# A float32 decoder trunk on Trainium2: token factors in the turning matmuls, norm weights in the split

## The chip, the cores and the metric

The kernel runs on one core of a Trainium2 chip. The metric is the device time of one execution in microseconds; lower is better. The core has TensorE (PE; its weight loads are shown apart as PEld), VectorE (DVE), ScalarE (ACT), GpSimd (POOL) and SyncE (SP), which here issues the DMAs.

## What is computed

Four residual layers over 512 tokens of 1024 channels, all in float32. Each layer has a token mixer (retention in layers 0 and 3, a Conformer convolution in layer 1, a short convolution in layer 2) and a squared-ReLU MLP, and each of these eight sublayers has an RMSNorm before and one after it:

```python
def rms_norm(x, g):
    xf = x.astype(F32)
    y = xf * lax.rsqrt(jnp.mean(xf * xf, axis=-1, keepdims=True) + RMS_EPS)
    return (y * g.astype(F32)).astype(x.dtype)

def squared_relu_mlp(x, w1, w2):
    return jnp.square(jax.nn.relu(x @ w1)) @ w2

    for i in range(DEPTH):
        kind, j = i % N_MIXERS, i // N_MIXERS
        h = rms_norm(x, norm_g[i, 0])
        if kind == 0:
            h = retention_mixer(h, positions, ret_w_in[j], ret_gn_g[j], ret_w_out[j])
        ...
        x = x + rms_norm(h, norm_g[i, 1])
        h = squared_relu_mlp(rms_norm(x, norm_g[i, 2]), mlp_w1[i], mlp_w2[i])
        x = x + rms_norm(h, norm_g[i, 3])
```

The matrix products keep float32 accuracy by splitting: every operand is a high part, rounded to the matmul's reduced float32, and a low part, the rest. A product is three matmuls (high by high, high by low, low by high).

## The kernel before

Weights come from DRAM in pieces of 128 x 1024 (`load`, tile `raw`, two buffers). `fetch_hi` rounds a piece on ScalarE into `whi`, and `fetch_lo` takes the rest on VectorE into `wlo` and asks for the next piece; seven pieces fit. `settle` makes fetches that are owed, at most as many as it is told.

The activations `x` lie with 128 tokens on the partitions, in four token blocks. A mixer or MLP needs them with the channels on the partitions, in `xin`, as high and low parts. The way from one sublayer to the next, a boundary, is `out_final`. Its first half makes channels 0 to 511 of the sublayer's output for all four token blocks. The second half is `block(b)` for token block b: 24 matmuls of 128x512 over four weight pieces. Around these calls the code writes out by hand what follows for each token block b: the evacuation of the product into `f` (`evac`), its square sum on ScalarE (`square`), `post_norm` (the factor 1/rms through `rstd`, two small GpSimd steps, and `fold`, the product of `f` and the norm weights on VectorE), `add` (x gets f times the factor), `pre_sum` (square sum of x and its factor), `pre_norm` (L434: x times the factor, by token, times the norm weights, by channel, into `bnd`), `transposes` (L445: eight 128x128 transposes of `bnd` on TensorE, into two PSUM banks) and `place` (the split of these banks into `xin`: L376 on ScalarE, L377 on VectorE, each twice 128x512).

`first_four` begins the next sublayer. It takes its first four weight pieces and makes the products for tokens 0 to 255 in eight steps of twelve 128x256 matmuls (two steps a piece); before step T2_AT it turns token block 2, before step T3_AT block 3. Then follow tokens 256 to 511. The last boundary of the program has no next sublayer. The start of the program (`build`) does the same work on the input x: twenty warm-up matmuls (`warm`, L237), then the turning of blocks 0 and 1, and blocks 2 and 3 within `first_four`. The norm weights arrive as a row that a DMA broadcasts to all partitions (`begin_boundary`).

Each engine runs its instructions in the order in which the code issues them: nothing is reordered except inside the Conformer mixer, which has a planner of its own. PSUM has eight banks, taken in turn.

Of the kernel before, what the change touches and what calls it, by code (L numbers as in the profile page):

```python
# [16 lines left out]
P = 128  # L17
# [27 lines left out]
T2_AT, T3_AT, FETCH_AT = 3, 7, 3  # L45
# [17 lines left out]
O_PH = O_INV + 1  # L63
# [137 lines left out]
class Trunk:  # L201
# [200 lines left out]
    def begin_boundary(self, post, pre):  # L402

        nc = self.nc
        t = self.big.tile([P, 4, D], F32, tag="bnd", name=self.nm("bnd"))
        if post is not None:
            nc.sync.dma_start(t[:, 0, :], self.norm_g[post[0], post[1]:post[1] + 1, :].broadcast_to([P, D]))
        if pre is not None:
            nc.sync.dma_start(t[:, 1, :], self.norm_g[pre[0], pre[1]:pre[1] + 1, :].broadcast_to([P, D]))
            self.xin = self.big.tile([P, 2, 8, S], F32R, tag="xin", name=self.nm("xin"))  # L410
        self.bnd = t
# [10 lines left out]
    def post_norm(self, b):  # L422
        self.r1[b] = self.rstd(self.sums[b])
        self.fold(b)
# [5 lines left out]
    def pre_sum(self, b):  # L430
        self.r2[b] = self.rstd([self.sumsq(self.x[:, b, :], self.bnd[:, 2 + b % 2, :])])

    def pre_norm(self, b):
        self.nc.vector.scalar_tensor_tensor(self.bnd[:, 2 + b % 2, :], self.x[:, b, :], self.r2[b],  # L434
                                            self.bnd[:, 1, :], op0=ALU.mult, op1=ALU.mult)

    def transposes(self, b):
        nc = self.nc
        h = self.bnd[:, 2 + b % 2, :]
        self.turned[b] = []  # L440
        for m in range(2):
            bk = self.bank().rearrange("p (k t) -> p k t", k=4)
            for k in range(4):
                d0 = (4 * m + k) * P
                nc.tensor.transpose(out=bk[:, k, :], in_=h[:, d0:d0 + P], identity=self.ident)  # L445
            self.turned[b].append(bk)

    def place(self, b):
        c = slice(b * P, (b + 1) * P)
        for m, bk in enumerate(self.turned.pop(b)):  # L450
            self.split(self.xin[:, 0, 4 * m:4 * m + 4, c], self.xin[:, 1, 4 * m:4 * m + 4, c], bk)
# [51 lines left out]
    def out_final(self, slots, mode, layer_end):  # L503
# [86 lines left out]
        self.transposes(0)  # L590
        square(2, 1)
        self.pre_norm(1)
        self.place(0)
        self.post_norm(2)
        block(3, range(3))
        self.transposes(1)
        self.add(2)
        self.place(1)
        if layer_end:
            layer_end(2)  # L600
        self.pre_sum(2)
        block(3, range(3, 4))
# [4 lines left out]
        post(3)  # L607

        def start(i):
            if i == T2_AT:  # L610
                self.transposes(2)
                if FETCH_AT & 1:
                    self.settle(1)
                self.place(2)
                self.pre_sum(3)
                self.pre_norm(3)
                if FETCH_AT & 2:
                    self.settle(1)
            elif i == T3_AT:
                self.transposes(3)  # L620
                self.place(3)
# [745 lines left out]
    def build(self):  # L1367
        tc, nc = self.tc, self.nc
        SP = bass.MemorySpace.PSUM if hasattr(bass, "MemorySpace") else bass.MemoryType.PSUM
        with tc.tile_pool(name="const", bufs=1) as cp, tc.tile_pool(name="big", bufs=1) as big, \  # L1370
# [13 lines left out]
            self.r1, self.r2, self.turned = {}, {}, {}  # L1384
# [3 lines left out]
            self.begin_boundary(None, (LAYERS[0], 0))  # L1388
            self.load()
# [4 lines left out]
            self.small = cp.tile([P, O_PH], F32, name="small")  # L1394
            nc.sync.dma_start(self.small, self.small_in[:, :O_PH])
# [8 lines left out]
            def head(b):  # L1404
                self.r2[b] = self.rstd([self.sumsq(self.x[:, b, :], self.f[:, b, :])])

            def start(i):
                if i == S2_AT:
                    self.transposes(2)
                    self.place(2)  # L1410
                    self.pre_norm(3)
                elif i == S3_AT:
                    self.transposes(3)
                    self.place(3)
# [11 lines left out]
            self.place(1)  # L1426
# [49 lines left out]
def lay_out(inputs):  # L1476
# [41 lines left out]
    small[:, O_PH:] = phases.reshape(-1, P).T  # L1518
    small[:, O_INV] = (10000.0 ** e.astype(np.float64)).astype(np.float32)
# [25 lines left out]
```

## Time and profile before

| | us |
|---|---|
| median of 3 runs | 2544.07 (2544.06 to 2546.12) |
| the profiled execution | 2545.85 |
| its span | 2544.1 |
| TensorE busy | 2516.4 |
| VectorE busy | 1652.9 |
| ScalarE busy | 1210.3 |
| GpSimd busy | 218.4 |

The span runs from the first to the last instruction of the profiled execution. Busy time is the sum of the stretches in which an engine has an instruction running; matmuls overlap, and their ends are modelled, so the distance between two starts says what a matmul costs in a row. The granted TensorE clock is 0.998 of full speed over the span.

### The profile page before, as it was taken

What the parts mean: (1) busy time and instruction counts of PE and PEld (TensorE: products, weight loads), DVE (VectorE), ACT (ScalarE), POOL (GpSimd) and SP (SyncE); (2) the same over time, 40 slices, a digit from 0 to 9 for tenths busy, and PEclk for the clock granted to TensorE, in tenths of its full rate; (3) what the DMA queues carried; (4) which work ended last, traced back from release to release, by engine and by line L of the source; (5) the groups of instructions that cost most, each with busy time, mean ns of one, the idle gap of its engine ahead of it and who ended that gap; (6) DMA issues with size and microseconds to landing.
All of it is one profiled execution on the core that took longest, in us unless ns stands there. A gap on an engine that the chain in (4) does not pass through costs nothing. (4 is left out here: it accounts for less than half of the span.)

```text
span 2544.1 us, 30985 instructions
## 1 busy us (share of the span) xinstructions
PE 2516.4 (99%) x12173; PEld 2124.6 (84%) x12173; DVE 1652.9 (65%) x2151; ACT 1210.3 (48%) x1829; POOL 218.4 (9%) x248
## 2 busy tenths in 40 slices
PE   9999999999999999999999999999999999999998
PEld 8888888888888788888888888888888888888887
DVE  7665346897758977677464476784646534677773
ACT  3543444555436656544332365444344334455542
POOL 1000002000027820000010100000100000200000
PEclk9999999999999999999999999999999999999999
DMA  4323234224423532332332333314322223421331
GB/s 160 104 88 109 78 127 172 97 102 170 153 92 108 188 128 100 124 133 91 116 100 99 108 116 133 133 52 155 128 79 80 95 90 106 162 106 67 133 124 67
DMA packets 85026, 290.94 MB, mean 114 GB/s; under 512 B 9488, under 2 KB 11280, under 8 KB 84880
## 3 DMA queue, kind: packets, MB, share of 16 engines
q1 hardware_dynamic: 84880, 288.96, 32.7%
q8 instruction: 95, 1.56, 0.2%
q14 instruction: 51, 0.42, 0.0%
HBM read 265.79 MB, written 21.50 MB: 113 GB/s over the span
## 5 line engine op out<-in xcount | busy, mean ns | idle before, releaser
L337 PE MATMUL bank<-xin,whi 128*128 128x512 f32 (+1 forms) x2112 | 753.3, 365 | 2.3 <-ACT xin L376 2.3
L338 PE MATMUL bank<-xin,wlo 128*128 128x512 f32 (+1 forms) x2112 | 750.3, 364 | 0.0
L282 DVE TENSOR_TENSOR wlo<-raw,whi 128x1024 fp32r<-128x1024 f32 x340 | 416.8, 1234 | 426.5 <-ACT whi L271 425.2
L271 ACT ACTIVATE whi<-raw 128x1024 fp32r<-128x1024 f32 x340 | 354.8, 1053 | 428.9 <-DMA raw<-wall 214.7
L340 PE MATMUL bank<-xin,whi 128*128 128x512 f32 (+1 forms) x2112 | 473.8, 364 | 3.2 <-DVE xin L377 3.2
L337 PEld LDWEIGHTS bank<-xin,whi 128*128 128x128 f32 x2112 | 398.9, 189 | 65.0 <-ACT xin L376 2.9
L338 PEld LDWEIGHTS bank<-xin,wlo 128*128 128x128 f32 x2112 | 399.0, 189 | 62.2
L340 PEld LDWEIGHTS bank<-xin,whi 128*128 128x128 f32 x2112 | 369.3, 189 | 67.1 <-DVE xin L377 4.8
L266 ACT ACTIVATE whi<-blk 128x1024 fp32r<-128x1024 f32 x168 | 174.5, 1053 | 123.1 <-DVE blk L303 117.0
L280 DVE TENSOR_TENSOR wlo<-blk,whi 128x1024 fp32r<-128x1024 f32 x168 | 204.8, 1221 | 19.9 <-ACT whi L266 18.7
L396 POOL TENSOR_SCALAR tiny<-tiny,tiny 128x1 f32<-128x1 f32 x32 | 52.3, 1635 | 1484.7 <-ACT tmp L415 1483.5
L1200 ACT ACTIVATE tmp<-bank 128x512 f32<-128x512 f32 x128 | 75.2, 588 | 133.0 <-PE bank L340 133.0
L1287 DVE TENSOR_TENSOR f<-f,bank 128x512 f32<-128x512 f32 x168 | 108.4, 681 | 0.0
L1067 POOL TENSOR_TENSOR pbuf<-pbuf 128x512 f32<-128x512 f32 x69 | 100.5, 1473 | 16.0 <-ACT pbuf L1064 12.7
L327 PE MATMUL bank<-whi,hid 128*128 128x512 f32 (+1 forms) x264 | 101.5, 385 | 0.0
L329 PE MATMUL bank<-whi,hid 128*128 128x512 f32 (+1 forms) x264 | 101.0, 383 | 0.0
L328 PE MATMUL bank<-wlo,hid 128*128 128x512 f32 (+1 forms) x264 | 101.0, 383 | 0.0
L327 PE MATMUL bank<-whi,y 128*128 128x512 f32 x256 | 99.9, 390 | 0.0
L327 PE MATMUL bank<-whi,xin 128*128 128x512 f32 x256 | 99.6, 389 | 0.0
L329 PE MATMUL bank<-whi,y 128*128 128x512 f32 x256 | 99.6, 389 | 0.0
L328 PE MATMUL bank<-wlo,y 128*128 128x512 f32 x256 | 99.6, 389 | 0.0
L328 PE MATMUL bank<-wlo,xin 128*128 128x512 f32 x256 | 99.6, 389 | 0.0
(224 smaller groups left out, 4135.6 us busy)
## 6 DMA issues: line engine op xcount, KB each, us to landing
raw<-wall SPq DMA_DIRECT2D x340, 512.0 KB, 3.3
blk<-wall SPq DMA_DIRECT2D x96, 512.0 KB, 5.4
park<-x SPq DMA_DIRECT2D x20, 512.0 KB, 2.6
x<-park SPq DMA_DIRECT2D x20, 512.0 KB, 4.5
bnd<-norm_g SPq DMA_DIRECT2D x16, 512.0 KB, 6.8
phase<-tmp SPq DMA_DIRECT2D x32, 256.0 KB, 2.0
x<-x_in SPq DMA_DIRECT2D x8, 512.0 KB, 6.5
whi<-phase SPq DMA_DIRECT2D x8, 512.0 KB, 6.9
```

The source lines that it names most:

```text
L266: nc.scalar.activation(hi, self.form_of(c, n), AF.Copy)
L271: nc.scalar.activation(hi, self.raws[i], AF.Copy)
L280: nc.vector.tensor_sub(lo, self.form_of(c, n), hi.bitcast(F32))
L282: nc.vector.tensor_sub(lo, self.raws.pop(i), hi.bitcast(F32))
L327: nc.tensor.matmul(out, ah, bh, start=start, stop=False)
L328: nc.tensor.matmul(out, ah, bl, start=False, stop=False)
L329: nc.tensor.matmul(out, al, bh, start=False, stop=stop)
L337: self.nc.tensor.matmul(out, wh[:, c], x, start=kt == 0, stop=False)
L338: self.nc.tensor.matmul(out, wl[:, c], x, start=False, stop=False)
L340: self.nc.tensor.matmul(out, wh[:, kt * P:(kt + 1) * P], self.xin[:, 1, kt, t0:t1], start=False, stop=kt == 7)
L1067: nc.gpsimd.tensor_tensor(accs[c], accs[c], pbuf[:, slot, :], op=ALU.add)
L1287: nc.vector.tensor_add(f, f, bank)
```

## The change

`pre_norm` no longer scales x. It multiplies the 128x128 identity by the factors of the 128 tokens and leaves this diagonal matrix in `bnd`. `transposes` becomes eight float32 matmuls with x as the stationary and the diagonal matrix as the moving operand, which turns and scales x at once. The norm weights are now one column per 128 channels in the table `small`, and `place` multiplies by them while it splits, now for two token blocks together: eight ScalarE and eight VectorE passes of 128x256, from four banks. `begin_boundary` loads no norm row for this any more, and the start loads `small` earlier. The order in `out_final` is new, and so are the steps of `first_four` at which blocks 2 and 3 are turned. `post_norm` calls `fold` ahead of `rstd`, and the factor of `pre_sum` moves into `pre_norm`.

```diff
-T2_AT, T3_AT, FETCH_AT = 3, 7, 3
+T2_AT, T3_AT = 2, 5
...
-            nc.sync.dma_start(t[:, 1, :], self.norm_g[pre[0], pre[1]:pre[1] + 1, :].broadcast_to([P, D]))
+
+            self.gain = O_G + 16 * pre[0] + 4 * pre[1]
...
     def post_norm(self, b):
+        self.fold(b)
         self.r1[b] = self.rstd(self.sums[b])
-        self.fold(b)
...
     def pre_sum(self, b):
-        self.r2[b] = self.rstd([self.sumsq(self.x[:, b, :], self.bnd[:, 2 + b % 2, :])])
+        self.sums2[b] = self.sumsq(self.x[:, b, :], self.bnd[:, 2, :])
 
     def pre_norm(self, b):
-        self.nc.vector.scalar_tensor_tensor(self.bnd[:, 2 + b % 2, :], self.x[:, b, :], self.r2[b],
-                                            self.bnd[:, 1, :], op0=ALU.mult, op1=ALU.mult)
+
+        r = self.rstd([self.sums2.pop(b)])
+        self.diag[b] = self.bnd[:, 3, b * P:(b + 1) * P]
+        self.nc.vector.tensor_scalar(self.diag[b], self.ident, r, None, op0=ALU.mult)
 
     def transposes(self, b):
-        nc = self.nc
-        h = self.bnd[:, 2 + b % 2, :]
-        self.turned[b] = []
-        for m in range(2):
-            bk = self.bank().rearrange("p (k t) -> p k t", k=4)
-            for k in range(4):
-                d0 = (4 * m + k) * P
-                nc.tensor.transpose(out=bk[:, k, :], in_=h[:, d0:d0 + P], identity=self.ident)
-            self.turned[b].append(bk)
-
-    def place(self, b):
-        c = slice(b * P, (b + 1) * P)
-        for m, bk in enumerate(self.turned.pop(b)):
-            self.split(self.xin[:, 0, 4 * m:4 * m + 4, c], self.xin[:, 1, 4 * m:4 * m + 4, c], bk)
+
+        if b % 2 == 0:
+            self.turned[b // 2] = [self.bank().rearrange("p (k t) -> p k t", k=2) for _ in range(4)]
+        t = slice(b % 2 * P, b % 2 * P + P)
+        for k in range(8):
+            self.nc.tensor.matmul(self.turned[b // 2][k // 2][:, k % 2, t], self.x[:, b, k * P:(k + 1) * P], self.diag[b],
+                                  start=True, stop=True)
+
+    def place(self, n):
+
+        c = slice(256 * n, 256 * n + 256)
+        for k in range(8):
+            v, g = self.turned[n][k // 2][:, k % 2, :], self.small[:, self.gain + k:self.gain + k + 1]
+            hi = self.xin[:, 0, k, c]
+            self.nc.scalar.activation(hi, v, AF.Copy, scale=g)
+            self.nc.vector.scalar_tensor_tensor(self.xin[:, 1, k, c], v, g, hi.bitcast(F32), op0=ALU.mult, op1=ALU.subtract)
...
         evac(2, 1, ends[2])
-        self.transposes(0)
         square(2, 1)
         self.pre_norm(1)
+        post(2)
+        self.pre_sum(2)
+        block(3, range(1))
+        self.transposes(0)
+        self.transposes(1)
         self.place(0)
-        self.post_norm(2)
-        block(3, range(3))
-        self.transposes(1)
-        self.add(2)
-        self.place(1)
-        if layer_end:
-            layer_end(2)
-        self.pre_sum(2)
-        block(3, range(3, 4))
+        block(3, range(1, 4))
         self.owed += 4
         evac(3, 1, ends[3])
         square(3, 1)
         self.pre_norm(2)
         post(3)
+        self.pre_sum(3)
...
             if i == T2_AT:
                 self.transposes(2)
-                if FETCH_AT & 1:
-                    self.settle(1)
-                self.place(2)
-                self.pre_sum(3)
+                self.settle(1)
                 self.pre_norm(3)
-                if FETCH_AT & 2:
-                    self.settle(1)
+                self.settle(1)
             elif i == T3_AT:
                 self.transposes(3)
-                self.place(3)
+                self.place(1)
```

What this makes of the engines' order is shown at the first inner boundary (retention of layer 0 to its MLP). First TensorE, where the turning of block 0 stands; the 128x512 rows belong to `block(2)` and `block(3)`. Before:

```order
L328 MATMUL bank_3180<-wlo_2984,y_2716 128x512
L329 MATMUL bank_3180<-whi_2983,y_2716 128x512
L445 MATMUL bank_3206<-ident,bnd_2945 128x128 x4
L445 MATMUL bank_3211<-ident,bnd_2945 128x128 x4
L327 MATMUL bank_3229<-whi_2842,y_2302 128x512
```

After, `bnd` being the diagonal:

```order
L447 MATMUL bank_3240<-bnd_2960,x_2954 128x128 x2
L447 MATMUL bank_3241<-bnd_2960,x_2954 128x128 x2
L447 MATMUL bank_3242<-bnd_2960,x_2954 128x128 x2
L447 MATMUL bank_3243<-bnd_2960,x_2954 128x128 x2
L447 MATMUL bank_3240<-bnd_2960,x_2954 128x128 x2
L447 MATMUL bank_3241<-bnd_2960,x_2954 128x128 x2
L447 MATMUL bank_3242<-bnd_2960,x_2954 128x128 x2
L447 MATMUL bank_3243<-bnd_2960,x_2954 128x128 x2
L328 MATMUL bank_3233<-whi_2899,y_2317 128x512
```

The turnings of blocks 0 and 1 now stand together, after the first six matmuls of block 3.

VectorE at the same place: L515 and L521 are evacuations, L420 and L422 folds, L428 and L430 adds, L282 and L283 low parts of weights. Before, from the scaling of block 1 on:

```order
L434 SCALAR_TENSOR_TENSOR bnd_2945<-x_2939,tiny_3177,bnd_2945 128x1024
L377 TENSOR_TENSOR xin_2948<-bank_3206,xin_2948 128x4x128
L377 TENSOR_TENSOR xin_2948<-bank_3211,xin_2948 128x4x128
L420 TENSOR_TENSOR f_2045<-f_2045,bnd_2945 128x1024
L428 SCALAR_TENSOR_TENSOR x_2939<-f_2045,tiny_3225,x_2939 128x1024
L377 TENSOR_TENSOR xin_2948<-bank_3248,xin_2948 128x4x128
L377 TENSOR_TENSOR xin_2948<-bank_3253,xin_2948 128x4x128
L515 TENSOR_TENSOR f_2045<-f_2045,bank_3229 128x512
L434 SCALAR_TENSOR_TENSOR bnd_2945<-x_2939,tiny_3267,bnd_2945 128x1024
```

After, from the diagonal of block 1 on, with the last diagonal (block 3) at the end:

```order
L439 TENSOR_SCALAR bnd_2960<-ident,tiny_3220 128x128
L422 TENSOR_TENSOR f_2060<-f_2060,bnd_2960 128x1024
L430 SCALAR_TENSOR_TENSOR x_2954<-f_2060,tiny_3226,x_2954 128x1024
...
L457 SCALAR_TENSOR_TENSOR xin_2962<-bank_3243,small,xin_2962 128x256 x2
L521 TENSOR_TENSOR f_2060<-f_2060,bank_3233 128x512
L439 TENSOR_SCALAR bnd_2960<-ident,tiny_3299 128x128
L422 TENSOR_TENSOR f_2060<-f_2060,bnd_2960 128x1024
L430 SCALAR_TENSOR_TENSOR x_2954<-f_2060,tiny_3305,x_2954 128x1024
L283 TENSOR_TENSOR wlo_3318<-raw_3061,whi_3317 128x1024
L283 TENSOR_TENSOR wlo_3364<-raw_3091,whi_3363 128x1024
L439 TENSOR_SCALAR bnd_2960<-ident,tiny_3370 128x128
```

The fold and the add of block 2 have moved ahead of the split of blocks 0 and 1, and the evacuation of block 3 is behind all of that split.

ScalarE: L415 and L417 are square sums (of `f` with 512 columns, of `x` with 1024), L271 and L272 roundings of weights. Before, from the square sum of x of block 2 on:

```order
L415 ACTIVATE bnd_2945,tiny_3264<-x_2939 128x1024
L415 ACTIVATE tmp_3277,tiny_3278<-f_2045 128x512
L271 ACTIVATE whi_3293<-raw_3047 128x1024
L271 ACTIVATE whi_3349<-raw_3077 128x1024
L376 ACTIVATE xin_2948<-bank_3339 128x4x128
L376 ACTIVATE xin_2948<-bank_3344 128x4x128
L415 ACTIVATE bnd_2945,tiny_3359<-x_2939 128x1024
```

After, from the same square sum on:

```order
L417 ACTIVATE bnd_2960,tiny_3231<-x_2954 128x1024
L456 ACTIVATE xin_2962<-bank_3240,small 128x256 x2
L456 ACTIVATE xin_2962<-bank_3241,small 128x256 x2
L456 ACTIVATE xin_2962<-bank_3242,small 128x256 x2
L456 ACTIVATE xin_2962<-bank_3243,small 128x256 x2
L417 ACTIVATE tmp_3295,tiny_3296<-f_2060 128x512
L417 ACTIVATE bnd_2960,tiny_3310<-x_2954 128x1024
L272 ACTIVATE whi_3317<-raw_3061 128x1024
L272 ACTIVATE whi_3363<-raw_3091 128x1024
```

The split of blocks 0 and 1 stands behind the square sum of block 2, and the two roundings behind that of block 3.

## Rows read from the trace of the kernel before

**Rows 1.** The page's first block: busy us, share of span, instructions.

```profile
PE 2516.4 (99%) x12173; PEld 2124.6 (84%) x12173; DVE 1652.9 (65%) x2151; ACT 1210.3 (48%) x1829; POOL 218.4 (9%) x248
```

**Rows 2.** TensorE by shape: line, op, out<-in, shapes, count; busy us, mean ns; idle.

```profile
L445 PE MATMUL bank<-ident,bnd 128*128 128x128 f32 x256 | 33.5, 274 | 8.3 <-DVE bnd L434 8.2
...
L718 PE MATMUL bank<-ends 128*128 128x128 f32 x32 | 4.8, 274 | 0.0
```

**Rows 3.** TensorE's timeline: start us, us to the last end, line, shapes, count.

```profile
409.64 1.03 PE L445 MATMUL bank<-ident,bnd 128*128 128x128 f32 x8
...
410.98 0.39 PE L329 MATMUL bank<-whi,y 128*128 128x512 f32 x1
411.21 0.39 PE L327 MATMUL bank<-whi,y 128*128 128x512 f32 x1
...
887.95 5.07 PE L237 MATMUL bank<-ident 128*128 128x128 f32 x44
```

**Rows 4.** By stretch: length, busy us (instructions) by engine, clock, DMA share, GB/s.

```profile
core 0: us, PE busy (x) PEld busy (x) DVE busy (x) ACT busy (x) POOL busy (x), PEclk, DMA share, GB/s
...
403.00:431.00 28.00, 27.15 (x200) 25.39 (x199) 20.93 (x23) 14.35 (x25) 8.77 (x12) 1.00 0.36 129
742.00:770.00 28.00, 25.22 (x185) 23.52 (x184) 20.92 (x23) 12.99 (x23) 7.68 (x13) 1.00 0.20 61
...
1449.00:1477.00 28.00, 26.55 (x195) 24.76 (x194) 20.05 (x21) 15.11 (x26) 8.85 (x12) 1.00 0.34 122
1788.00:1820.00 32.00, 28.67 (x200) 26.83 (x200) 21.97 (x25) 13.87 (x23) 8.28 (x11) 0.95 0.41 140
```

**Rows 5.** TensorE's timeline at the first inner boundary; in brackets idle time and releaser.

```profile
413.30 0.74 PE L340 MATMUL bank<-xin,whi 128*128 128x256 f32 x4 [0.30 <-DVE xin L377]
...
422.90 0.64 PE L340 MATMUL bank<-xin,whi 128*128 128x256 f32 x4
424.09 1.06 PE L445 MATMUL bank<-ident,bnd 128*128 128x128 f32 x8 [0.56 <-DVE bnd L434]
```

**Rows 6.** The same boundary, timelines of ScalarE, VectorE and GpSimd.

```profile
405.51 1.06 ACT L415 ACTIVATE bnd<-x 128x1024 f32<-128x1024 f32 x1 [4.64 <-DVE x L428]
...
415.16 1.99 ACT L271 ACTIVATE whi<-raw 128x1024 fp32r<-128x1024 f32 x2
...
401.01 1.28 DVE L434 SCALAR_TENSOR_TENSOR bnd<-x,tiny,bnd 128x1024 f32<-128x1024 f32 x1 [0.89 <-POOL tiny L399]
402.21 1.22 DVE L420 TENSOR_TENSOR f<-f,bnd 128x1024 f32<-128x1024 f32 x1
...
419.20 2.35 DVE L282 TENSOR_TENSOR wlo<-raw,whi 128x1024 fp32r<-128x1024 f32 x2
...
401.07 2.44 POOL L396 TENSOR_SCALAR tiny<-tiny,tiny 128x1 f32<-128x1 f32 x1
```

**Rows 7.** VectorE and ScalarE by shape, the nearest forms to the new ones.

```profile
L377 DVE TENSOR_TENSOR own<-tmp,own 128x256 fp32r<-128x256 f32 x96 | 40.5, 421 | 19.8 <-ACT own L376 19.4
...
L773 DVE SCALAR_TENSOR_TENSOR tmp<-tmp,small,tmp 128x512 f32<-128x512 f32 x32 | 24.1, 752 | 2.1
...
L640 DVE CAST ones<-tmp 128x128 fp32r<-128x128 f32 x2 | 0.5, 227 | 0.1
...
L696 ACT ACTIVATE v<-tmp,tiny 128x512 fp32r<-128x512 f32 x24 | 15.6, 720 | 0.0
```

**Rows 8.** The start of the program, timeline of TensorE and VectorE.

```profile
1.34 6.78 PE L237 MATMUL bank<-ident 128*128 128x128 f32 x40 [1.34 <-POOL ident masks.py:199]
...
8.67 2.48 DVE L434 SCALAR_TENSOR_TENSOR bnd<-x,tiny,bnd 128x1024 f32<-128x1024 f32 x2 [7.76 <-DMA bnd<-norm_g]
...
12.55 0.19 PEld L337 LDWEIGHTS bank<-xin,whi 128*128 128x128 f32 x1 [0.49 <-ACT xin L376]
...
22.99 1.06 PE L445 MATMUL bank<-ident,bnd 128*128 128x128 f32 x8
```

**Rows 9.** The boundary from the MLP of layer 2 to layer 3, timelines.

```profile
1811.76 1.06 ACT L271 ACTIVATE whi<-raw 128x1024 fp32r<-128x1024 f32 x1 [6.95 <-DMA raw<-wall]
...
1813.36 0.39 PE L337 MATMUL bank<-xin,whi 128*128 128x256 f32 x1 [2.02 <-ACT xin L376]
```

More of the change, by code (lines that the diff above doesn't have):

```diff
@@ L62 @@
 O_INV = O_SC + 24
-O_PH = O_INV + 1
+O_G = O_INV + 1
+O_PH = O_G + 16 * DEPTH
 N_SM = O_PH + 64 * len(POLY)
@@ L1383, in build @@
             self.x = big.tile([P, 4, D], F32, tag="x", name="x0")
-            self.r1, self.r2, self.turned = {}, {}, {}
+            self.r1, self.sums2, self.diag, self.turned = {}, {}, {}, {}
             self.early = big.tile([P, 4, D], F32, tag="h", bufs=2, name="early")
@@ L1388, in build @@
             self.begin_boundary(None, (LAYERS[0], 0))
+            self.small = cp.tile([P, O_PH], F32, name="small")
+            nc.sync.dma_start(self.small, self.small_in[:, :O_PH])
             self.load()
@@ L1393, in build @@
                 self.load()
-            self.small = cp.tile([P, O_PH], F32, name="small")
-            nc.sync.dma_start(self.small, self.small_in[:, :O_PH])
             self.phases, self.dram = {}, dram
@@ L1404, in head @@
             def head(b):
-                self.r2[b] = self.rstd([self.sumsq(self.x[:, b, :], self.f[:, b, :])])
+                self.sums2[b] = self.sumsq(self.x[:, b, :], self.f[:, b, :])
             def start(i):
@@ L1409, in start @@
                     self.transposes(2)
-                    self.place(2)
                     self.pre_norm(3)
@@ L1413, in start @@
                     self.transposes(3)
-                    self.place(3)
+                    self.place(1)
                     self.fetch()
@@ L1425, in build @@
             self.place(0)
-            self.place(1)
             self.fetch()
@@ L1518, in lay_out @@
     small[:, O_PH:] = phases.reshape(-1, P).T
+    small[:, O_G:O_G + 16 * DEPTH] = cols(a["norm_g"][:, ::2])
     small[:, O_INV] = (10000.0 ** e.astype(np.float64)).astype(np.float32)
```

## The prediction

> **What bounds the kernel now.** I read the page's first block, then TensorE's instructions by shape, then stretches of its timeline, then a table by stretch, and last the queues of the other engines at one sublayer boundary. TensorE is busy for 2516.4 us of a span of 2544.1 us [rows 1]. So all its idle time together is 27.7 us, and some of that lies in places that the change doesn't touch, such as the end of the program. Anything that adds TensorE work adds it to the end, unless it fits into one of these gaps. The first question is therefore not what the boundaries wait for, but what the new matmuls cost on TensorE.
>
> **The price of a turning matmul.** Before, each 128x128 piece of a normalised block is turned by one transpose: 8 boundaries (the start and seven inside) x 4 blocks x 8 pieces = 256, and the trace has 256 instructions [rows 2]. Eight in a row take 1.03 us from first start to last end [rows 3]; one is 0.274 us long [rows 2], so the spacing is (1.03 - 0.27) / 7 = 0.109 us. After, each is a real float32 matmul, x as the stationary operand and the diagonal of factors as the moving one. The trace has such matmuls. warm() asks for 22 of them and the row has 44 instructions, in 5.07 us [rows 3]; the spacing is (5.07 - 0.27) / 43 = 0.112 us, so one matmul is two instructions, 0.223 us. The product of the two `ends` tiles, with two different data operands and each its own weights, shows the same doubling: 16 calls in the code (2 layers, 4 heads, 2 halves), 32 instructions [rows 2]. The surcharge is 0.223 - 0.109 = 0.114 us, and 256 x 0.114 = **29.3 us**, 3.66 us at each boundary. I see no reason for a float32 matmul of this shape to be an exception, so I take this as near certain. It is more than the 27.7 us of idle time in the whole span: even if the change removed every gap of TensorE, it would not pay.
>
> The Trainium skill speaks against this edit too: "Perfetto Trace Analysis", section Transposes, asks that a logical transpose use the transpose and not a standard matmul, since the transpose skips the arithmetic. It gives no figure; the rows above give one, a factor of 2.05.
>
> **What the boundaries can give back.** The table by stretch [rows 4] gives TensorE's idle time as stretch minus busy: 0.85 us at 403, 2.78 at 742, 1.45 at 1449 and 3.33 at 1788; the other three (931, 1269, 2192) are like the first, 0.85 to 0.93. The seven make 11.1 us. The modelled end of a matmul hides a little more: at the first inner boundary the turning after the last 128x256 matmuls is shown as 0.56 us late, but the four before it start at 422.90 and are 0.12 us apart, so it was due at 423.38 and starts at 424.09, 0.71 us late [rows 5]. Two waits a boundary make 7 x 2 x 0.15 = 2.1 us. In the stretch at 1788 the granted clock is 0.95 of 32 us, another 1.6 us. In all about 14.9 us; and each group of turnings leaves the next matmul 0.09 us late, of which there is one less per boundary, 0.6 us. **15.5 us is the most** that seven boundaries can give.
>
> What is left of it depends on the new order. I lay it out at the first inner boundary, from the end of token block 2 (404.67). TensorE: the first weight piece of block 3, 6 x 0.227 = 1.36 (128x512 matmuls stand 0.227 us apart [rows 3]); two turnings, 32 x 0.112 = 3.57; the rest of block 3, 4.09; two steps of first_four, 2.88 (a step is twelve 128x256 matmuls at 0.12); a turning, 1.79; three steps, 4.32. So the third turning group of the tail, that of block 3, is due at +18.0 us.
>
> The other engines: the scaling pass L434 of 1.28 us becomes a 128x128 product, for which 0.23 us of a 128x128 cast stands [rows 7]. That lets the fold of block 1 start about 1.0 us earlier, and the GpSimd step L396, which sat from 401.07 until the end of the two VectorE passes beside it [rows 6], ends 1.0 us earlier too. So the square sum of block 1, before at 405.51 [rows 6], runs at 404.5, its factor is there at 406.6 and the second diagonal at +2.2: in time, as its turning is due at +3.2. Then the fold of block 2 (1.22), GpSimd behind it, the add (1.28) and the square sum of block 2 (1.06) end at +6.6. On ScalarE place(0) is queued behind this square sum. It is 8 passes of 128x256 on ScalarE and 8 on VectorE, with a column factor. None of this form is in the trace. Bounds: 0.42 us without a factor (L377, 128x256), 0.72 and 0.75 us with one at twice the width (L696 on ScalarE, L773) [rows 7]. In a row they overlap a little; I take a step of 0.36 us on both, near the lower row, because the width is its. place(0) then ends on ScalarE at +9.5 and on VectorE at +10.0, and the first high parts at +7: first_four starts at +9.0 **without a wait**, where before it waited 0.46 us. That wait goes.
>
> But on VectorE the last evacuation is queued behind place(0): it ends at +10.7 instead of about +9.7. Behind it stand diagonal 2, the fold of block 3, GpSimd, the add and the square sum: +15.3. On ScalarE the two weight roundings now stand **behind** that square sum (before they stood ahead of it, and were done by 417.15 [rows 6]); on VectorE the two low parts (2.35 us before [rows 6]) stand ahead of the last diagonal. Roundings end at +16.3 and +17.3, low parts at +17.5 and +18.7, diagonal 3 at +18.9. Due at +18.0, so TensorE waits **0.9 us** there, where before it waited 0.71. Waiting instructions hold up only fetches that are not needed before step 6, and place(1), whose result is first used at +25 and which is done by then.
>
> At five boundaries I leave 0.9 us. At the one before the conformer (742) a small VectorE fill and a ScalarE pass come ahead of the roundings: 1.1 us of 2.8. At 1788 the old loss came from a late weight load: ScalarE waited until 1811.76 for it with the last split behind it, and TensorE 2.02 us for that split [rows 9]. TensorE now comes there some 2 us later, so most is hidden; but place(1) gives its high parts at 0.36 us a piece where TensorE takes one per 0.24 us, and the low parts end 1.0 us late: 1.9 us. Left: 5 x 0.9 + 1.1 + 1.9 = 7.5 us. **Given back: 15.5 - 7.5 = 8.0 us.**
>
> **The start.** The first scaling pass waits 7.76 us for the norm weights to land [rows 8]; after, only x and the factor are needed. But the warm-up matmuls hold TensorE until 8.1 [rows 8], so the first two turning groups run from 8.1 to 11.7, and the first product starts at 11.7 instead of 12.55 [rows 8]. The weight roundings of piece 1 are behind place(0), which costs some 1.0 us of this; the last turning group then ends at 25.0, against 24.0 before [rows 8]. So of the 3.66 us added here, 2.7 us are hidden. The small table now lands ahead of the first weights, in the place of the broadcast norm row, which is larger. The eight broadcast loads less, and the post_norm steps written in another order, change no queue that TensorE waits for: nothing.
>
> **Sum.** 29.3 - 8.0 - 2.7 = **+18.6 us**. The profiled execution is 2545.85 us with a span of 2544.1; the median of the runs is 2544.07, and a difference carries over: 2544.07 + 18.6 = 2562.7.
>
> **Rivals.**
> 1. The waits go entirely: place() runs at the lower bound or better and the last evacuation isn't late. Then 29.3 - 15.5 - 2.7 = +11, 2555 us. For it: the late diagonal misses by about a microsecond only. Against: the two low parts ahead of it are seen to take 2.35 us.
> 2. place() is dear: if each pass cost what a 128x512 one with a factor costs (0.75 us), VectorE would be 8 x 0.39 = 3.1 us later at each boundary, 7 x 3.1 = 22 us more: 2585 us. Against: L377 at 128x256 costs 0.42 us, so cost falls with width.
> 3. Faster: the diagonal matmul is issued as one pass at the transpose's spacing. Then there is no surcharge and 8.0 + 2.7 us are gained: 2533 us. It decides from a surcharge under 10.7 / 256 = 0.042 us. Against: both kinds of float32 matmul in the rows are doubled.
> 4. A turning matmul costs four transposes, 0.436 us: 256 x 0.327 = 83.7, less 10.7: 2617 us. Against: the rows measure the ratio at 2.05. The Trainium skill ("TensorE: Matmul & The Clock Gate", Terms) has a transpose mode that is 4x faster for FP32; the trace differs.
>
> **How the numbers follow.** Forecast with a wait left at most boundaries (+13 to +27): 0.56. Rival 1, +8 to +13: 0.26. Rival 2, in part or in whole (over +27): 0.10. Rival 3: 0.04. Rival 4: 0.01. A hidden surcharge that leaves it within 0.2%: 0.03. About 0.2% (5 us) is what a measurement of this kernel can tell from no change. Faster 0.04, same 0.03, slower 0.93. The range 2552 to 2571 takes in the forecast, rival 1 and the near end of rival 2.
>
> **What would show it.** Right: 512 instructions on the turning line, 0.112 us apart, TensorE busy some 29 us longer with its first-four wait on VectorE gone and a wait of about 0.9 us before the turnings of block 3. Wrong: 256 instructions (rival 3), a spacing over 0.2 us (rival 4), no wait at the turnings (rival 1), or waits on xin longer than 1 us (rival 2).

## The result and the profile after

The changed kernel takes 2610.65 us (median of 4 runs, 2609.14 to 2611.88); the kernel before takes 2544.28 on the same chip. The ratio is 1.0259, with a 95% interval of 1.0241 to 1.0277. The prediction had 2562.7 with a range up to 2571. The sign was right, and the size was not: +66 us instead of +18.6. The profiled execution took 2611.49 us, with a span of 2609.7 us, 65.6 us more than before.

The first block of the page of after, which answers to [rows 1], and the group of the turning matmuls by shape, which answers to [rows 2]:

```profile
PE 2561.5 (98%) x12429; PEld 2163.3 (83%) x12429; DVE 1641.9 (63%) x2215; ACT 1231.5 (47%) x1893; POOL 200.2 (8%) x248
```

```profile
L447 PE MATMUL bank<-bnd,x 128*128 128x128 f32 x512 | 66.8, 290 | 19.2 <-DVE bnd L439 19.2
```

There are 256 instructions more, as predicted. But TensorE's idle time grew from 27.7 to 48.2 us, where the prediction let it shrink, and its busy time grew by 45 us and not by 29. The list of TensorE's waits in after (us in total, times, longest us) says for whom it waits:

```profile
PE bank L447 <- DVE bnd L439: 19.2, 13, 2.6
PE bank L338 <- ACT xin L456: 10.2, 25, 0.6
...
PE bank L328 <- ACT own L377: 1.7, 1, 1.7
```

Before, the largest entry was 8.2 us (the waits of L445 in [rows 2]). TensorE's timeline in after at the first inner boundary, which answers to [rows 5] and [rows 3], shows where these waits lie (start us, us to the last end, line, count, in brackets idle time and releaser):

```profile
413.08 3.73 PE L447 MATMUL bank<-bnd,x 128*128 128x128 f32 x32
...
422.77 0.38 PE L338 MATMUL bank<-xin,whi 128*128 128x256 f32 x1 [0.21 <-ACT xin L456]
...
424.19 0.38 PE L338 MATMUL bank<-xin,whi 128*128 128x256 f32 x1 [0.55 <-ACT xin L456]
...
425.50 2.05 PE L447 MATMUL bank<-bnd,x 128*128 128x128 f32 x16 [0.34 <-DVE bnd L439]
...
434.30 3.39 PE L447 MATMUL bank<-bnd,x 128*128 128x128 f32 x16 [2.44 <-DVE bnd L439]
```

The first row gives the spacing: (3.73 - 0.28) / 31 = 0.111 us, the predicted price. Then come four waits where the prediction had one. The last row has a second loss: 16 instructions took 3.39 us there and 2.05 us in the row above. The table by stretch (as [rows 4]: length, busy us by engine, then the granted clock, the DMA share and GB/s) shows why. At this boundary the engine ran at the lower level, 1.2 GHz, after it had stood still for 2.44 us (not at every boundary: see the last section):

```profile
434.00:436.00 2.00, 1.71 (x10) 1.71 (x11) 0.24 (x2) 0.00 (x0) 0.00 (x0) 0.69 0.90 272
436.00:438.00 2.00, 2.00 (x11) 2.00 (x11) 0.61 (x1) 1.42 (x2) 0.00 (x0) 0.50 0.74 236
438.00:440.00 2.00, 2.00 (x18) 2.00 (x18) 1.46 (x4) 0.84 (x2) 0.00 (x0) 0.96 0.20 61
```

The cause stands in the timelines of ScalarE and VectorE at the same boundary, which answer to [rows 6]. L456 and L457 are the two passes of place():

```profile
418.40 0.46 ACT L456 ACTIVATE xin<-bank,small 128x256 fp32r<-128x256 f32 x1
419.41 0.84 ACT L456 ACTIVATE xin<-bank,small 128x256 fp32r<-128x256 f32 x2 [0.55 <-DVE xin L457]
420.83 0.84 ACT L456 ACTIVATE xin<-bank,small 128x256 fp32r<-128x256 f32 x2 [0.58 <-DVE xin L457]
422.25 0.84 ACT L456 ACTIVATE xin<-bank,small 128x256 fp32r<-128x256 f32 x2 [0.58 <-DVE xin L457]
423.66 0.47 ACT L456 ACTIVATE xin<-bank,small 128x256 fp32r<-128x256 f32 x1 [0.58 <-DVE xin L457]
```

```profile
418.89 0.48 DVE L457 SCALAR_TENSOR_TENSOR xin<-bank,small,xin 128x256 fp32r<-128x256 f32 x1 [1.64 <-ACT xin L456]
419.92 0.88 DVE L457 SCALAR_TENSOR_TENSOR xin<-bank,small,xin 128x256 fp32r<-128x256 f32 x2 [0.54 <-ACT xin L456]
...
424.17 0.48 DVE L457 SCALAR_TENSOR_TENSOR xin<-bank,small,xin 128x256 fp32r<-128x256 f32 x1 [0.54 <-ACT xin L456]
424.57 0.68 DVE L521 TENSOR_TENSOR f<-f,bank 128x512 f32<-128x512 f32 x1
425.17 0.28 DVE L439 TENSOR_SCALAR bnd<-ident,tiny 128x128 f32<-128x128 f32 x1
426.10 1.23 DVE L422 TENSOR_TENSOR f<-f,bnd 128x1024 f32<-128x1024 f32 x1 [0.65 <-ACT tmp L417]
428.18 1.28 DVE L430 SCALAR_TENSOR_TENSOR x<-f,tiny,x 128x1024 f32<-128x1024 f32 x1 [0.85 <-POOL tiny L400]
431.68 2.36 DVE L283 TENSOR_TENSOR wlo<-raw,whi 128x1024 fp32r<-128x1024 f32 x2 [2.23 <-ACT whi L272]
433.96 0.28 DVE L439 TENSOR_SCALAR bnd<-ident,tiny 128x128 f32<-128x128 f32 x1
```

A pass takes 0.46 us on ScalarE and 0.48 us on VectorE, about as long as assumed. But every second pass of ScalarE waits 0.55 to 0.58 us **for VectorE**, and VectorE waits as long for ScalarE. The step from piece to piece is (423.66 - 418.40) / 7 = 0.75 us, not 0.36. Two pieces share a bank: piece k lies in bank k // 2. In the built program ScalarE's first pass on a bank waits for TensorE, and its second one carries a wait for VectorE's first pass on that bank (here on the second bank of the program's first place()):

```
L456 ACTIVATE xin_96<-bank_144,small 128x256 [waits PE_49]
L456 ACTIVATE xin_96<-bank_144,small 128x256 [waits DVE_49]
```

So the two engines take turns on a bank. place(0) takes 6.2 us (418.40 to 424.65), and everything behind it on VectorE is late: the last evacuation, the second diagonal, the fold of block 3 and the last diagonal.

### The profile page after: what moved, and what is told of

Its sections match the earlier page's. It is cut to its first block, busy times and chain, and to the rows that moved or that the text cites. A ratio compares the mean times of both kernels' runs of the same rounds, so it can differ in the third digit from the quotient of the medians.

```text
span 2609.7 us, 31593 instructions
## 1 busy us (share of the span) xinstructions
PE 2561.5 (98%) x12429; PEld 2163.3 (83%) x12429; DVE 1641.9 (63%) x2215; ACT 1231.5 (47%) x1893; POOL 200.2 (8%) x248
## 4 chain that ended last, share of the span: by engine, by line
PE 81%; DVE 7%; ACT 5%; POOL 4%; issue 1%; DMA 1%; POOLq 0%; DVEq 0%; ACTq 0%; SPq 0%
PE bank L341 14%; PE bank L338 14%; PE bank L339 14%; PE bank L330 13%; PE bank L328 13%; PE bank L329 13%; DVE xin L457 2%; POOL pbuf L1066 2%; POOL tiny L397 1%; DVE x L430 1%; DVE bank L1087 1%; ACT xin L456 1%; ACT bnd L417 1%; DVE wlo L283 1%; POOL tiny L400 1%
## 5 line engine op out<-in xcount | busy, mean ns | idle before, releaser
L338 PE MATMUL bank<-xin,whi 128*128 128x512 f32 (+1 forms) x2112 | 761.9, 368 | 10.3 <-ACT xin L456 10.2
L283 DVE TENSOR_TENSOR wlo<-raw,whi 128x1024 fp32r<-128x1024 f32 x340 | 417.6, 1236 | 447.2 <-ACT whi L272 442.4
L272 ACT ACTIVATE whi<-raw 128x1024 fp32r<-128x1024 f32 x340 | 354.8, 1053 | 420.0 <-DMA raw<-wall 223.1
L338 PEld LDWEIGHTS bank<-xin,whi 128*128 128x128 f32 x2112 | 400.9, 190 | 79.7 <-ACT xin L456 15.7
L397 POOL TENSOR_SCALAR tiny<-tiny,tiny 128x1 f32<-128x1 f32 x32 | 41.6, 1299 | 1555.7 <-ACT tmp L417 1554.5
L1066 POOL TENSOR_TENSOR pbuf<-pbuf 128x512 f32<-128x512 f32 x69 | 100.5, 1470 | 23.5 <-ACT pbuf L1063 20.3
```

The source lines that it names most:

```text
L272: nc.scalar.activation(hi, self.raws[i], AF.Copy)
L283: nc.vector.tensor_sub(lo, self.raws.pop(i), hi.bitcast(F32))
L338: self.nc.tensor.matmul(out, wh[:, c], x, start=kt == 0, stop=False)
L1066: nc.gpsimd.tensor_tensor(accs[c], accs[c], pbuf[:, slot, :], op=ALU.add)
```

## The experiments

For the tables I add up, over the matmuls from 22 us before a boundary's first turning to 22 us after its last, by how much each one starts later than 0.227 us (512 columns), 0.120 us (256) or 0.110 us (128) after the one before it. These **late starts** hold waits and lower clock, but not the price. Before they are 16.0 us at the seven inner boundaries and 6.0 us at the start; after, 45.9 and 7.5 us.

**1. The banks.** In the changed kernel, neighbouring pieces go to different banks; nothing else differs (only the indices of the two lines are shown).

```
-  self.turned[b // 2][k // 2][:, k % 2, t]
+  self.turned[b // 2][k % 4][:, k // 4, t]
...
-  v = self.turned[n][k // 2][:, k % 2, :]
+  v = self.turned[n][k % 4][:, k // 4, :]
```

> The changed kernel with one thing changed: the eight turned pieces go to the four PSUM banks in turn (piece k to bank k mod 4) instead of two neighbours to a bank, and the split reads them there. Theory A (the split is slow because ScalarE's second pass on a bank waits for VectorE's first pass on the same bank, so that the two engines take turns): the split of two token blocks takes about 3.4 us instead of 6.2, the waits at the head of the first four pieces and at the second turning go, the wait before the third falls from 2.6 to about 1.5 us, and the time falls by about 35 us to 2575. Theory B (the new order of the blocks makes the waits, whatever the split takes): no change, 2610.

Measured: 2578.87 us, ratio 1.0125 (1.011 to 1.014), so 32 us of the loss are gone. place(0) in this kernel, on ScalarE:

```profile
413.59 3.01 ACT L456 ACTIVATE xin<-bank,small 128x256 fp32r<-128x256 f32 x8
```

The step is (3.01 - 0.46) / 7 = 0.364 us, the prediction's own figure. No wait of L338 for ScalarE's xin is left in the list of waits, and the late starts at the inner boundaries fall from 45.9 to 20.7 us. Theory A holds: the turns on a bank cost about half of the 66 us (some 3.6 of the 32 us lie in the MLP of layer 0, see experiment 7). What is left is one wait a boundary, longer than the 1.5 us that A expected:

```profile
PE bank L447 <- DVE bnd L439: 13.6, 7, 2.1
```

**2. The price alone.** The kernel before, its 256 transposes written as real matmuls by the identity.

```
-  nc.tensor.transpose(out=bk[:, k, :], in_=h[:, d0:d0 + P], identity=self.ident)
+  nc.tensor.matmul(bk[:, k, :], h[:, d0:d0 + P], self.ident, start=True, stop=True)
```

> The kernel before with one thing changed: each transpose is a real float32 matmul by the identity. The price alone, in the old order. Theory A (surcharge of 0.114 us each, 29.3 us in all, of which the waits of 0.7 to 2.6 us before the last turning hide some 9): 2564. If the price were all of the loss: 2610. If a matmul cost no more than a transpose: 2544.

Measured: 2558.35 us, ratio 1.0045 (1.003 to 1.006), +11.5 us beside the 2546.89 us of before in these runs. TensorE has 12429 instructions, so the price is there; but the late starts fall from 16.0 to 1.6 us at the inner boundaries and from 6.0 to 4.2 us at the start. The longer turnings fill the gaps that TensorE had: 29.2 - 14.4 - 1.8 = 13 us, close to the 11.5 measured; theory A, at 2564, had them hide only some 9 us. The prediction let the new order close the gaps; here TensorE closes them by being late itself, and the same gap can't be closed twice.

**3. The order, undone in part.** The changed kernel with the turnings of blocks 0 and 1 around block 3 as before, the split of both where that of block 1 stood, and the square sum of block 2 behind it; pieces in pairs as in the change. Two things of the new order stay: the add of block 2 ahead of the split, and the steps of first_four.

```
         evac(2, 1, ends[2])
+        self.transposes(0)
         square(2, 1)
         self.pre_norm(1)
-        post(2)
+        self.post_norm(2)
+        block(3, range(3))
+        self.transposes(1)
+        self.add(2)
+        self.place(0)
...
         self.pre_sum(2)
-        block(3, range(1))
-        self.transposes(0)
-        self.transposes(1)
-        self.place(0)
-        block(3, range(1, 4))
+        block(3, range(3, 4))
```

> The changed kernel with the old order around block 3: turning of block 0 after block 2, three quarters of block 3, turning of block 1, the split of both, the last quarter; the add and square sum of block 2 behind that. Banks as in the changed kernel. Theory A: the split still takes 6.2 us and now starts later against its first use, so the waits move to the first four pieces and grow: about 2630. Theory B (the order makes the waits): 2575 to 2585.

Measured: 2608.57 us, ratio 1.0244 (1.0227 to 1.0261), the same as the changed kernel; both theories missed. To see whether the turns on the banks cover the order up, the same edit was made with the banks of experiment 1:

> The changed kernel with the banks as in e1_banks and the old order of the work around block 3: the first turning group directly behind block 2, three weight pieces of block 3, the second group, then place(0), the add of block 2 and its square sum behind it. In e4_order, with two neighbouring pieces in a bank, the two orders gave the same time. Theory A (the alternation on the banks covered up the order; with it gone the order decides, since in the old one place(0) stands ahead of the add of block 2, which comes 3 us later, and with it the diagonals of blocks 2 and 3): slower than e1_banks by 1.5 to 3 us at a boundary, 2590 to 2600 us. Rival B (the order is worth nothing here): 2576 to 2582 us.

Measured: 2576.51 us, ratio 1.0126 (1.011 to 1.0141), as in experiment 1. TensorE waits twice at each boundary here and once there, with nearly the same sum (15.7 and 13.6 us in the lists of waits). The time is rival B's. But theory A was not put to the test: it rests on an add of block 2 behind place(0), and the edit leaves it ahead, as VectorE's timeline in this run shows:

```profile
411.57 1.28 DVE L430 SCALAR_TENSOR_TENSOR x<-f,tiny,x 128x1024 f32<-128x1024 f32 x1 [0.76 <-POOL tiny L400]
415.04 3.22 DVE L457 SCALAR_TENSOR_TENSOR xin<-bank,small,xin 128x256 fp32r<-128x256 f32 x8 [2.19 <-ACT xin L456]
```

So the two runs show that the places of the first two turnings, of the split and of the square sum of block 2 gain or cost nothing that can be measured, in either layout of the banks. What the place of the add is worth, and that of the steps of first_four, is not shown.

**4. The last diagonal ahead of a fetch.** Experiment 1's kernel, and in first_four's step 2:

```
                 self.transposes(2)
-                self.settle(1)
                 self.pre_norm(3)
-                self.settle(1)
+                self.settle(2)
```

> The changed kernel with the pieces spread over the banks as in e1_banks, and one thing more: in first_four's step 2 the last diagonal (block 3) is issued ahead of the two weight fetches, so that VectorE makes it before the two low parts of 2.36 us and not behind them. Theory A (the rest of the loss is this one wait, 2.0 to 2.3 us before the third turning group at each of seven boundaries, 13.6 us in the list of waits, because the low parts stand ahead of the diagonal): the factor is there at 424.3 in e1_banks and the turning is due at 424.7, so the waits go; 2578.9 - 14 to 17 (some of the slow-clock stretches behind them too) = about 2563 us, ratio 1.007, which is the place that the prediction gave. Rival B (the chain from the square of block 3 to its factor is late whatever stands in VectorE's queue, or the fetches pushed behind the diagonal are late for their use): the wait stays at over 1 us at most boundaries or comes back on L339 or L328, 2572 us or more.

Measured: 2567.88 us, ratio 1.0091 (1.0074 to 1.0107). The waits on the diagonal fall from 13.6 to 5.4 us (7 times, 1.0 at most), the late starts from 20.7 to 7.9 us. It gains 11 us where A expected 14 to 17. In its trace the MLP of layer 0 also loses 3.4 us more than in experiment 1's (see experiment 7). VectorE's timeline shows what is left at the boundary:

```profile
418.06 1.22 DVE L422 TENSOR_TENSOR f<-f,bnd 128x1024 f32<-128x1024 f32 x1 [0.65 <-ACT tmp L417]
420.13 1.28 DVE L430 SCALAR_TENSOR_TENSOR x<-f,tiny,x 128x1024 f32<-128x1024 f32 x1 [0.84 <-POOL tiny L400]
423.64 1.22 DVE L283 TENSOR_TENSOR wlo<-raw,whi 128x1024 fp32r<-128x1024 f32 x1 [2.23 <-ACT whi L272]
424.78 0.28 DVE L439 TENSOR_SCALAR bnd<-ident,tiny 128x128 f32<-128x128 f32 x1
```

One low part still stands ahead of the diagonal (the fetch at the head of first_four, which the edit doesn't move). And the fold waits for the square sum L417, because it overwrites f in place, which the square sum reads.

**5. The fold out of place.** Experiment 4's kernel; at the inner boundaries the fold writes into the quarter of bnd that the norm row left free, and the add reads from there.

```
-        self.nc.vector.tensor_mul(f, f, self.bnd[:, 0, cols])
+        out = f if self.next_pre is None else self.bnd[:, 1, cols]
+        self.nc.vector.tensor_mul(out, f, self.bnd[:, 0, cols])
```

> e5_norm3 with one thing more: the fold of a block at the inner boundaries writes into a free quarter of bnd, from which the add reads, and not back into f. So it need not wait until ScalarE's square sum has read f; in e5_norm3 as in the changed kernel VectorE waits 0.65 us there, and the GpSimd step of the same block runs beside the fold and takes 1.32 us. Theory A (this wait is the second step that the prediction left out, and what is left before the third turning group, 0.8 to 1.1 us at each boundary, goes with it): last diagonal about 0.9 us earlier, waits on bnd down from 5.4 us to under 1.5, 2567.9 - 6 = about 2562 us. Rival B (the chain runs over the square sum and GpSimd's factor, which don't get earlier, so the add is no earlier and the wait stays): 2566 to 2569 us.

Measured: 2558.82 us, ratio 1.0052 (1.0035 to 1.0069), lower than A's 2562. No wait on a diagonal is left; the late starts at the inner boundaries are 0.6 us. The same row as above:

```profile
416.72 1.22 DVE L423 TENSOR_TENSOR bnd<-f,bnd 128x1024 f32<-128x1024 f32 x1
```

It starts right behind the diagonal (416.52, 0.28 long). The add waits for GpSimd's factor in both kernels, as rival B said; but GpSimd's step beside the fold got shorter, here first in experiment 4's kernel and then in this one:

```profile
418.13 1.32 POOL L397 TENSOR_SCALAR tiny<-tiny,tiny 128x1 f32<-128x1 f32 x1 [4.17 <-ACT tmp L417]
```

```profile
417.52 0.58 POOL L397 TENSOR_SCALAR tiny<-tiny,tiny 128x1 f32<-128x1 f32 x1 [4.17 <-ACT tmp L417]
```

In both it ends 0.16 to 0.17 us after the fold does (419.45 after 419.28, and 418.10 after 417.94). So the earlier fold brings the factor, and with it the add, 0.75 us closer to the square sum. With every gap at the inner boundaries closed, the sum is 29.2 - 15.4 (inner boundaries) - 2.1 (start) = 11.7 us; the span is 12.5 us longer than before. This is rival 1's case, all waits at the inner boundaries gone, and it is still slower than the kernel before.

**6. The price taken away, with a longer pass on VectorE.** Experiment 4's kernel, turned by transposes: VectorE multiplies the factor into a copy of the block, as before, and the weights stay in the split. So two things differ: TensorE has less to do, and the scaling pass is 128x1024 again.

```
-        self.diag[b] = self.bnd[:, 3, b * P:(b + 1) * P]
-        self.nc.vector.tensor_scalar(self.diag[b], self.ident, r, None, op0=ALU.mult)
+        self.diag[b] = self.bnd[:, 1 + 2 * (b % 2), :]
+        self.nc.vector.tensor_scalar(self.diag[b], self.x[:, b, :], r, None, op0=ALU.mult)
...
+            self.nc.tensor.transpose(out=..., in_=self.diag[b][:, k * P:(k + 1) * P], identity=self.ident)
```

> e5_norm3 without the price of the real matmul: the factor of a token is multiplied into a copy of the block on VectorE (128x1024) and the copy is turned by 256 single-instruction transposes; weights in the split, banks and order as in e5_norm3. Theory A (the price of the matmul is paid at the boundaries and in part fills waits there: TensorE comes 3.7 us a boundary earlier and VectorE has about 1 us more to do for each block, so waits of 1 to 2 us come back before the first product and of 2 to 3 us before the third turning group): TensorE busy about 2517 us, 12173 instructions, waits on bnd and xin of 15 to 30 us in all, 2545 to 2562 us, no better than the kernel before. Rival B (price and waits are independent): e5_norm3's time less 29, about 2534 us.

Measured: 2572.31 us, ratio 1.0107 (1.0092 to 1.0122): 4 us **slower** than with the price, which neither theory had (A's upper end was 2562). TensorE is busy 19 us less (2524.1 against 2543.5) and waits more:

```profile
PE bank L447 <- DVE bnd L439: 28.2, 21, 2.5
```

The late starts at the inner boundaries are 41.5 us instead of 7.9. The scaling pass of block 3 takes 0.74 us, against 0.28 in experiment 4's rows:

```profile
423.18 0.74 DVE L439 TENSOR_SCALAR bnd<-x,tiny 128x1024 f32<-128x1024 f32 x1
```

Its turning starts 20.3 us after the first matmul of block 3, against 18.9 in experiment 4's kernel. In this layout the boundary ends with VectorE's chain and not with TensorE's work: the saving on TensorE is turned into waiting, and the longer scaling passes make the chain longer. No run has the saving without the longer passes (one with transposes by the diagonal itself gave no result), so how the 4 us divide is not shown.

**7. A side effect in the MLP of layer 0.** Set beside before matmul by matmul, the changed kernel's trace loses 3.8 us more between 426 and 471 us of before, far from a boundary. The row of ScalarE there, before and after:

```profile
443.66 0.31 ACT L376 ACTIVATE taps<-tmp 128x128 fp32r<-128x128 f32 x1 [6.52 <-DMA tmp<-small]
```

```profile
461.89 0.31 ACT L377 ACTIVATE taps<-tmp 128x128 fp32r<-128x128 f32 x1 [8.94 <-DMA tmp<-small]
```

ScalarE stands still until a small table has landed. The wait and the loss go together in the traces, one execution each: 6.76 us and a loss of 0.2 us in experiment 1's kernel, 8.62 and 3.6 us in experiment 4's, 8.22 and 1.7 us in experiment 5's. On experiment 5's kernel, its use was put off by one step:

```
         nc.sync.dma_start(t, self.small_in[:, O_PH:O_PH + n])
         yield
+        yield
         self.split(taps[:, 0], taps[:, 1], t)
```

> e9_fold with one thing more: in layer 0's MLP, where the tap table is loaded in one step of its chunks and split by ScalarE in the next, the split comes one step later (one more yield between the load and the split). In the traces ScalarE waits for this load 6.5 us in the kernel before and 8.2 to 8.9 us in the changed kernel and its variants, and TensorE, which waits 0.3 us for the products behind it before, waits 2.4 us for them in the changed kernel (and runs some instructions at the lower clock there). Theory A (this load is the cause of the 3.6 us that the changed kernel and its variants lose between 459 and 471 us of the kernel before): the waits on own in that place go, 2558.8 - 3 to 4 = 2555 to 2556 us. Rival B (VectorE's or ScalarE's queue is late there by itself): 2558 to 2560 us.

Measured: 2557.08 us, ratio 1.0047 (1.003 to 1.0063). TensorE's two waits on own, a tile that its matmuls there read (1.0 and 0.7 us in experiment 5's kernel), are gone and ScalarE's wait is 5.35 us, so the table is the cause of the waits (why it lands later in the changed kernel is open); the gain of 1.7 us is smaller than expected and within the intervals of the two.

**8. The lesson put into the kernel before.** The last norm ahead of a fetch, without the change (two conditions that are always true are left out of the lines):

```
                 self.transposes(2)
+                self.pre_sum(3)
+                self.pre_norm(3)
                 self.settle(1)
                 self.place(2)
-                self.pre_sum(3)
-                self.pre_norm(3)
                 self.settle(1)
```

> The kernel before with one thing moved: in first_four's step 3 the square sum and the scaling pass of block 3 are issued ahead of the fetch and of place(2). Theory A (the wait before its last turning group, 0.7 us at five boundaries, 2.65 at 742 and 1.1 at 1788, has the same cause as in the changed kernel, low parts and splits queued ahead of the last factor): scaling pass 1.3 to 2.1 us earlier, waits on bnd down from 8.2 us to under 2, about 2538 us, ratio 0.997. Rival B (what is pushed back, place(2) and the fetches, becomes late for the second half of first_four): 2544 us or more.

Measured: 2541.7 us, ratio 0.999 (0.998 to 0.9999), less than expected. The waits on the last scaling pass fall from 8.2 to 2.0 us, but in the profiled execution the products of the MLP of layer 0 came 4 us later, as in 7. So both edits were put together:

> e8_norm3 (the kernel before with the norm of block 3 ahead of the fetches and of place(2)) with the later split of the tap table from e10_taps. In e8_norm3's trace the boundaries together lose 3.8 us less than before, but the products of layer 0's MLP come 4 us later, as in the changed kernel. Theory A (both are to be had, the loss in the MLP comes from the tap table): waits on own gone, waits on bnd under 2 us, 2539 to 2541 us, ratio 0.998. Rival B (what is gained at the boundaries comes back elsewhere, as in e8_norm3's trace): 2543 to 2546 us.

Measured: 2540.05 us (11 runs), ratio 0.9979 (0.997 to 0.9988). This version beats both kernels, by 5 us (0.2%) against before. It doesn't get all: at the boundary of [rows 9] TensorE's wait for the last split is now 3.1 us instead of 2.02.

## Why the prediction was right and wrong

**The price** was right: 512 instructions, 0.111 us apart, 256 x 0.114 = 29.2 us. Rivals 3 and 4 fall with it. So was the remark that closing every gap would not pay: experiment 5 closes them at the inner boundaries, and stays 0.5% above before.

**place()** is the step that failed. "I take a step of 0.36 us on both" holds only where neighbouring pieces lie in different banks (0.364 us in experiment 1). As the change lays them out, it is 0.75 us, and that costs about 32 us (experiment 1): a pass waits for the other engine's pass on the same bank. That was to be read ahead of time from the shape of the change (two pieces in a bank, two engines that read it) and from the waits in the built program. I bounded the duration of one pass and took for granted that the passes of the two engines overlap. Rival 2 has the right 0.75 us for the wrong reason, a dear pass, and priced it too low, at 22 us; I gave it 0.10 and drew the range at its near end.

**"first_four starts without a wait"** held for its first products and failed behind them for the same reason: in its first two steps TensorE waits twice for the split, 0.21 and 0.55 us in the rows. That place(1) "is done by then" failed too: at three boundaries TensorE waits about 1 us for it (rows in the last section). **"TensorE waits 0.9 us there"**, at the third turning, was 2.44 us, with 0.34 us at the second ahead of it. Beside place(), a second step was left out: the fold of block 3 waits for the square sum of f (0.65 us), and GpSimd's step of 1.33 us beside it comes later too. It appears in no row of before, since VectorE had the scaling pass to do in between; experiment 5 shows it. Experiment 1's kernel, which has the predicted step, shows what this is worth: it still takes 16 us more than the forecast. At the first inner boundary the third turning is due at +18.0 us, as laid out, but diagonal 3 is ready at +20.0 and not at +18.9. Over seven boundaries that is about 8 us; lower clock at three of them adds about 5. The prediction also had nothing for the lower clock after such a wait, though it counted that loss at 1788 before [rows 4].

**The sum**, in late starts: the seven boundaries were to give 8.0 us back and cost 45.9 - 16.0 = 29.9 us; the start was to hide 2.7 us and cost 1.5 us. With the price of 29.2 us and the 3.8 us of the MLP that is 64.4 us of the 65.6 by which the span grew; 1.2 us stay unexplained.

**The new order** was given the credit for closing gaps. Experiment 3 shows no measurable effect of the part of it that it undoes, in either layout of the banks, and experiment 2 shows that the gaps of before close by the longer turnings alone.

**The skill's rule.** The Trainium skill, "Perfetto Trace Analysis", section Transposes, asks for the transpose in place of a standard matmul, and the traces agree as to the price (0.109 us against 0.223 us). Experiment 6 adds that following it inside this layout, with the longer scaling pass that it needs there, gains nothing, since the other engines' chain sets the end.

## What to carry to other kernels

Before two engines are given alternate pieces of one PSUM tile, look in the built program whether the second pass on it waits for the other engine's first; spreading neighbouring pieces over banks halved the step here. A surcharge on the bounding engine is not simply added: it closes that engine's waits (29.2 us cost 11.5 alone), and a saving can open them (29 us less work on TensorE, bought with 0.46 us more for each scaling pass on VectorE, left the kernel 4 us slower). Where an engine waits for the last small result of a chain, look first at what stands ahead of that result in the producer's queue: moving one norm ahead of a weight fetch gave 11 us here and, with a later use of one small load, 5 us in the kernel before.

## What the runs showed of the hardware

I hadn't expected that a wait of 2.44 us can cost more than itself. After the one at 434.30 the granted clock is 0.69, 0.50 and 0.96 in three stretches of 2 us (the rows above), which is 0.31 + 0.50 + 0.04 of 2 us each, 1.7 us.

It doesn't do so every time. In the changed kernel the third turning waits 2.35 to 2.63 us at all seven inner boundaries, and the clock falls behind four of these waits. At 981.53, after the same 2.44 us, it stays at 1.00 (last row), and TensorE waits for the second split instead:

```profile
981.53 2.05 PE L447 MATMUL bank<-bnd,x 128*128 128x128 f32 x16 [2.44 <-DVE bnd L439]
...
989.55 0.38 PE L338 MATMUL bank<-xin,whi 128*128 128x256 f32 x1 [0.47 <-ACT xin L456]
...
990.97 0.39 PE L338 MATMUL bank<-xin,whi 128*128 128x256 f32 x1 [0.55 <-ACT xin L456]
```

```profile
983.00:985.00 2.00, 2.00 (x20) 2.00 (x19) 0.47 (x1) 1.42 (x2) 0.00 (x0) 1.00 0.71 236
```

Behind the third turning both kinds of boundary lose nearly the same in late starts, 1.8 to 2.2 us where the clock fell and 1.7 to 1.8 us where it did not: in the changed kernel the lower clock takes up time that TensorE would have waited. In experiment 1's kernel there is no wait for the second split, and the clock shows by itself: the three boundaries at which it fell lose 1.7 us behind the third turning (at 770 us, after a late start of 2.25 us, it is 0.78 and 0.50 in the two stretches behind it), the other four 0.14 us.
